# Split-buffer pairs and raw tiles of a weight stream: three and six, or four and four

## The chip, the cores and the metric

The kernel runs on one core of one Trainium2 chip. The metric is the device time of one execution in microseconds, the median of the runs shown.

## The reference

One layer of a hybrid trunk works on two request groups that share the weights: 128 context tokens and 256 latent tokens, 384 token columns of width 2048 in all, in float32. Cut to what matters:

```python
mod = silu(c) @ w_mod + b_mod                # one vector for each group, 6 x 2048 columns
h = rmsnorm(x, g) * (1 + sc_a) + sh_a        # modulated by parts of mod
parts = h @ w_in                             # 16,944 columns: three branches and their gates
merged = g0 * (y_m @ w_br_m) + g1 * (y_r @ w_br_r) + g2 * (y_s @ w_br_s)   # mLSTM, retention, SSD
x = x + g_a * (merged @ w_out)
h = rmsnorm(x, g) * (1 + sc_f) + sh_f
x = x + g_f * (square(relu(h @ w_ff1)) @ w_ff2)   # width 8192
y = rmsnorm(x, final_norm_g)
```

The three scans (y_m, y_r, y_s) also return their final states for the context group.

## The kernel before

Every large product streams its weights from HBM in raw tiles of 128 partitions x 1024 float32 values (512 KB). A weight is split in two halves that TensorE takes at its fast rate: whi is the rounded weight (`rnd`, line 88, ScalarE), wlo is what rounding left (`tt`, line 91, VectorE: raw minus whi). The activations are split in the same way, and each product is three matmuls (high by high, high by low, low by high; lines 201 to 203 and 209 to 211).

The work is a list of units (`unit_list`), filled by `strip` (line 114): a unit is one raw tile of weights, 4 row blocks by 256 columns (kind A, 24 matmuls of 384 columns) or 2 row blocks by 512 columns (kind B5, 18 matmuls of 512 columns). Four to eight units, two for the branch matrices, make a block that fills PSUM banks and is evacuated one unit later (`flush_evac`). Two further streams run in the background. `bg` holds generators for the scans, one step after each unit. And w_mod, whose parts for later stages aren't needed at the start, is mixed into the same list: `strip` adds `tune["rate"]` to a counter for each unit and, each time the counter passes 1, puts a modulation tile (kind M) behind the unit, 128 in all. Eight of them make a quarter of one part of mod (512 columns), after which the counter is set back by 3 in place of 1. The rate is 0.65 in the first stage of `run_units` (lines 915 to 939, 25 tiles), between 0.25 and 0.65 from there to the end of the retention stage (31 tiles), 0.65 in the branch stage (line 1446, 44 tiles), 0.5 in w_out (10 tiles) and 0.8 at the start of w_ff1 (18 tiles).

A modulation tile isn't split. `mod_tile` (line 328) queues `first`, which adds two rows' worth of products to macc on VectorE (line 333; four instructions where `mx` is 2), and `second`, which takes the other products through ScalarE (line 342) and POOL (line 343, an addition to macc). Only the last of these sets the raw tile free (`raw_done`). At a quarter's end `mod_end` (line 350) sums macc on TensorE, and `mod_begin` puts a memset of macc (POOL) and the loads of the next bias (SP, line 321) in front of what is queued. `pop_mods` takes a few of these steps after each unit; a None in the queue ends its turn.

`run_units` (line 213) sets the order by hand, since every engine runs its instructions in the order of the program. For unit i it emits the splits of the units up to i + SPB - 1 (line 217), then issues raw tiles, then the unit's matmuls, a background step, modulation steps and evacuations. `emit_raws` (line 135) lists raws on the SP queue up to `pos["used"] + RAWB`, where `pos["used"]` is the first raw, in list order, that isn't free yet. Where a split needs a raw that isn't listed, `emit_splits` takes modulation steps until it is:

```python
while ri not in raws:      # lines 148 to 150
    pop_mods(1)
    emit_raws()
```

RAWB is also the number of buffers of the raw tiles (line 82), SPB that of whi and of wlo (lines 153 and 154). A buffer given to a new tile makes the new tile's first writer wait, on the chip, for the last reader of the one that was released first. A raw tile, a whi and a wlo have 4 KB per partition each.

Before `run_units` a start stage (lines 399 to 597) makes the modulated input and the third branch gate from 32 raw tiles of w_in and 32 tiles of w_mod of 1 MB (`mraw`, four buffers of their own), in groups; `st_half(i, 1)` emits a split ahead (line 511), and `st_split(0)` and `st_split(1)` come before the loop (lines 555 and 558).

Of the kernel before, what the change touches and what calls it, by code (L numbers as in the profile page):

```python
# [46 lines left out]
def hybrid_step(ctx: ExitStack, tc: tile.TileContext, cpack, x_prompt, x_sample, c, state_mlstm_C,  # L47
# [3 lines left out]
                final_norm_g, y_prompt, y_sample, new_C, new_n, new_m, new_ret, new_ssd):  # L51
    nc = tc.nc
    act, dve, pool, pe, sp = nc.scalar, nc.vector, nc.gpsimd, nc.tensor, nc.sync
    RAWB, SPB = 6, 3

    class Pool:
        def __init__(self, name, side="left", space=None):
# [20 lines left out]
    def gbank(name="gb"):  # L78
        return psum([128, 512], name, bufs=4, tag="g")
# [7 lines left out]
    def rnd(out, in_, **kw):  # L87
        act.activation(out=out, in_=in_, func=AF.Copy, **kw)  # L88

    def tt(eng, out, a, b, op):  # L90
        eng.tensor_tensor(out=out, in0=a, in1=b, op=op)  # L91
# [7 lines left out]
    def mm(out, l, r, start=True, stop=True):  # L99
        pe.matmul(out, l, r, start=start, stop=stop)  # L100
# [323 lines left out]
    def st_pump():  # L424
        while todo and held[todo[0][0]] < (4 if todo[0][0] == "m" else RAWB):
            kind, key, src, nk = todo.popleft()
            held[kind] += 1
            t = start([128, 2048], "mraw", bufs=4) if kind == "m" else raw_tile()
            sp.dma_start(out=r3(t, nk), in_=src.rearrange("(k p) f -> p k f", p=128))
            (mraw if kind == "m" else wraw)[key] = r3(t, nk)  # L430
# [6 lines left out]
    def st_gemv(g, m):  # L437
        if g >= NG:
            return
        n = groups[g][1]  # L440
        if m == 1:
            mps[g] = bank("gemv")
        o = 0 if m else 128 * n
        for hf in range(n):
            t = mraw.pop((g, m, hf))
            nk = KT // n
            for kk in range(nk):
                k = nk * hf + kk
                q = k % 4
                mm(mps[g][32 * q:32 * q + 32, o:o + 128 * n], cs[:, k], t[:, kk], k < 4, k >= 12)  # L450
            held["m"] -= 1
        if m == 0:
            p = mps.pop(g)
            mps[g] = macc[:, g % 2, 0:256 * n]
            act.copy(out=mps[g], in_=p[:, 0:256 * n])
            if g + 1 < NG:
                st_scale(g + 1)
        st_pump()
# [14 lines left out]
    def st_build(g):  # L473
        if g >= NG:
            return
        k0, n = groups[g]
        for k in range(k0, k0 + n):
            p = bank()
            for c_ in range(3):
                tp(p[:, 128 * c_:128 * c_ + 128], xt[:, c_, 128 * k:128 * k + 128])  # L480
            t = start([128, T], "ht", bufs=2)
            for v, a, b in GRP:
                if k % 2 or n == 1:
                    act.activation(out=t[:, a:b], in_=p[:, a:b], func=AF.Identity, scale=scA[:, k, v:v + 1],
                                   bias=shA[:, k, v:v + 1])
                else:
                    dve.tensor_scalar(out=t[:, a:b], in0=p[:, a:b], scalar1=scA[:, k, v:v + 1],
                                      scalar2=shA[:, k, v:v + 1], op0=ALU.mult, op1=ALU.add)
            rnd(hhi[:, k], t)
            tt(dve, hlo[:, k], t, hhi[:, k].bitcast(F32), ALU.subtract)  # L490

    def st_split(i, eng=dve):
        if i >= len(units):
            return
        g, u = units[i]
        n = groups[g][1]
        w = 1024 // n
        s_ = wraw.pop((g, u))
        hi = strm([128, n, w], "whi", bufs=SPB, dt=F32R)
        lo = strm([128, n, w], "wlo", bufs=SPB, dt=F32R)  # L500
        rnd(hi, s_)
        tt(eng, lo, s_, hi.bitcast(F32), ALU.subtract)
        wsp[i] = (hi, lo)
        held["w"] -= 1
        st_pump()

    def st_half(i, half):
        g, u = units[i]
        k0, n = groups[g]
        if half:  # L510
            st_split(i + 2)
        wh, wl = wsp[i]
        nc_ = 8 // n
        for c_ in range(nc_ // 2 * half, nc_ // 2 * half + nc_ // 2):
            p = gbank()[:, 0:T]
            q = slice(128 * c_, 128 * c_ + 128)
            for kk in range(n):
                k = k0 + kk
                mm(p, wh[:, kk, q], hhi[:, k], kk == 0, False)
                mm(p, wh[:, kk, q], hlo[:, k], False, False)  # L520
                mm(p, wl[:, kk, q], hhi[:, k], False, kk == n - 1)
            a = acc[:, nc_ * u + c_]
            if g == 0:
                act.copy(out=a, in_=p)
            elif n == 1 and c_ % 2:
                t = start([128, T], "at", bufs=2)
                act.copy(out=t, in_=p)  # L527
                tt(pool, a, a, t, ALU.add)
            else:
                tt(dve, a, a, p, ALU.add)  # L530
                if g == NG - 1:
                    act.activation(out=a, in_=a, func=AF.Sigmoid)
# [23 lines left out]
    st_vec(0)  # L556
    st_build(0)
    st_split(1)
    def st_m1(g):
        st_gemv(g, 1)  # L560

    def st_m0(g):
        st_gemv(g, 0)

    nxt = {1: {0: (st_m1, st_m0), 1: (st_vec, st_build)}, 2: {1: (st_m1,), 3: (st_m0,), 4: (st_vec,), 5: (st_build,)}}
    i = 0
    for g, (k0, n) in enumerate(groups):
# [21 lines left out]
        for h_ in range(4 * n):  # L589
            if g == NG - 1 and h_ in (4, 6):  # L590
                g_prep(h_ // 2 - 2)
            st_half(i + h_ // 2, h_ % 2)
            if later_loads:
                later_loads.popleft()()
            for f in nxt[n].get(h_, ()):
                f(g + 1)
# [1140 lines left out]
```

## Time and profile before

| | us |
|---|---|
| median of 3 runs | 2814.65 |
| the runs | 2812.88 to 2815.4 |
| the profiled execution | 2816.29 |
| its span, from the first to the last instruction | 2814.5 |

The profile is of one execution. Times are us from the start of the span. Engines: PE is TensorE's matmul, PEld its weight load, DVE VectorE, ACT ScalarE, POOL GpSimd, SP the queue that issues the transfers (SPq its sequencer). A row names a line of the kernel, an operation, the tiles written and read, and in brackets or behind `<-` what ended the idle time before it. TensorE's mean granted clock is 0.993 of full speed.

### The profile page before, as it was taken

The page shows a single profiled execution, that of the slowest core. Times are in us where ns is not written, and L with a number is a line of the kernel's source. Part 1 is how long each engine was busy: PE and PEld are TensorE (multiplying, and loading weights), DVE is VectorE, ACT ScalarE, POOL GpSimd, SP SyncE. Part 2 cuts the span into 40 slices and gives each one's busy share as a digit, 9 for nine tenths or more (in the row PEclk, how much of TensorE's full clock was granted, in tenths as well). Part 3 has the DMA queues.
Part 4 walks back from the last instruction along what each step waited for, and adds up shares of the span by engine and source line. Part 5 has one row for each costly group of instructions (what it writes and reads, how often), then busy time and mean ns, then how long its engine had stood idle before and what let it go on. Part 6 is the DMA issues. An engine that isn't in the chain of part 4 may idle for free. (4 is left out here: it accounts for less than half of the span.)

```text
span 2814.5 us, 38093 instructions
## 1 busy us (share of the span) xinstructions
PE 2725.1 (97%) x15023; PEld 2501.5 (89%) x15023; DVE 1561.0 (55%) x1883; ACT 1155.5 (41%) x1708; POOL 754.8 (27%) x588
## 2 busy tenths in 40 slices
PE   6999999999999999999999998999999999999998
PEld 5899988899998988989999877988899899889987
DVE  3666566645765465567876756773343334334434
ACT  5333444546643343544444445452233233323333
POOL 3200233512251111235766442441100100010012
PEclk9999999999999999999999999999999999999999
DMA  9955555545755555466666653664443344344442
GB/s 316 293 194 173 149 170 158 168 141 154 213 151 158 154 179 166 142 191 205 195 201 188 226 161 115 187 203 140 129 127 128 128 128 127 128 128 127 127 144 103
DMA packets 377835, 465.54 MB, mean 165 GB/s; under 512 B 20980, under 2 KB 277128, under 8 KB 376504
## 3 DMA queue, kind: packets, MB, share of 16 engines
q1 hardware_dynamic: 377656, 463.10, 53.8%
q8 instruction: 118, 1.93, 0.3%
q14 instruction: 61, 0.50, 0.1%
HBM read 449.47 MB, written 13.57 MB: 165 GB/s over the span
## 5 line engine op out<-in xcount | busy, mean ns | idle before, releaser
L91 DVE TENSOR_TENSOR wlo<-raw,whi 128x1024 fp32r<-128x1024 f32 x599 | 819.5, 1373 | 955.3 <-ACT whi L88 946.1
L88 ACT ACTIVATE whi<-raw 128x1024 fp32r<-128x1024 f32 x600 | 632.5, 1058 | 1005.8 <-PE sb L100 465.6
L100 PE MATMUL gb<-hhi,whi 128*128 128x384 f32 x1600 | 552.1, 345 | 13.5 <-ACT at L527 5.3
L100 PE MATMUL gb<-hhi,wlo 128*128 128x384 f32 x1600 | 541.3, 338 | 11.8 <-DVE wlo L91 11.7
L100 PE MATMUL gb<-hlo,whi 128*128 128x384 f32 x1600 | 538.8, 337 | 0.0
L91 POOL TENSOR_TENSOR macc<-macc,raw 128x512 f32<-128x512 f32 x194 | 324.1, 1670 | 354.0 <-issue 247.1
L100 PE MATMUL gb<-h2l,whi 128*128 128x384 f32 x1024 | 344.5, 336 | 5.1 <-DVE h2l L1544 5.0
L100 PE MATMUL gb<-h2i,wlo 128*128 128x384 f32 x1024 | 344.1, 336 | 4.1 <-DVE wlo L91 4.1
L100 PE MATMUL gb<-h2i,whi 128*128 128x384 f32 x1024 | 344.1, 336 | 2.2 <-ACT h2i L1540 1.5
L333 DVE SCALAR_TENSOR_TENSOR macc<-raw,cs,macc 128x512 f32<-128x512 f32 x318 | 326.0, 1033 | 7.0 <-DMA macc<-in_b_mod_dram 1.1
L100 PEld LDWEIGHTS gb<-hhi,whi 128*128 128x128 f32 x1600 | 303.4, 190 | 29.3 <-issue 8.4
L100 PEld LDWEIGHTS gb<-hhi,wlo 128*128 128x128 f32 x1600 | 303.1, 189 | 17.7 <-DVE wlo L91 17.6
L100 PEld LDWEIGHTS gb<-hlo,whi 128*128 128x128 f32 x1600 | 303.1, 189 | 1.3 <-issue 0.5
L91 POOL TENSOR_TENSOR x<-x,t 128x512 f32<-128x512 f32 x45 | 71.7, 1623 | 801.7 <-DVE t L91 801.7
L100 PEld LDWEIGHTS gb<-h2l,whi 128*128 128x128 f32 x1024 | 193.2, 189 | 8.0 <-DVE h2l L1544 7.9
L100 PE MATMUL gb<-whi,ahi 128*128 128x512 f32 x512 | 199.3, 389 | 0.0
L100 PE MATMUL gb<-wlo,ahi 128*128 128x512 f32 x512 | 199.3, 389 | 0.0
L100 PE MATMUL gb<-whi,alo 128*128 128x512 f32 x512 | 199.2, 389 | 0.0
L100 PEld LDWEIGHTS gb<-h2i,wlo 128*128 128x128 f32 x1024 | 193.3, 189 | 5.7 <-DVE wlo L91 5.7
L100 PEld LDWEIGHTS gb<-h2i,whi 128*128 128x128 f32 x1024 | 193.3, 189 | 4.8 <-ACT h2i L1540 1.8
L342 ACT ACTIVATE raw<-raw,cs 128x512 f32<-128x512 f32 x194 | 133.8, 716 | 68.3 <-DVE macc L333 63.0
L100 PE MATMUL gb<-yhi,whi 128*128 128x384 f32 x384 | 129.1, 336 | 1.3 <-ACT yhi L88 1.3
(413 smaller groups left out, 3899.1 us busy)
## 6 DMA issues: line engine op xcount, KB each, us to landing
raw<-in_w_in_dram SPq DMA_DIRECT2D x264, 512.0 KB
raw<-in_w_ff_dram SPq DMA_DIRECT2D x256, 512.0 KB
raw<-in_w_mod_dram SPq DMA_DIRECT2D x128, 512.0 KB
mraw<-in_w_mod_dram SPq DMA_DIRECT2D x32, 1024.0 KB
raw<-in_w_out_dram SPq DMA_DIRECT2D x32, 512.0 KB
raw<-in_w_br_r_dram SPq DMA_DIRECT2D x16, 512.0 KB
raw<-in_w_br_m_dram SPq DMA_DIRECT2D x16, 512.0 KB
raw<-in_w_br_s_dram SPq DMA_DIRECT2D x16, 512.0 KB
```

What stands on the lines that cost most here:

```text
L88: act.activation(out=out, in_=in_, func=AF.Copy, **kw)
L91: eng.tensor_tensor(out=out, in0=a, in1=b, op=op)
L100: pe.matmul(out, l, r, start=start, stop=stop)
L333: dve.scalar_tensor_tensor(out=macc[:, v], in0=t[:, kk], scalar=cs[:, 2 * r + kk, v:v + 1], in1=macc[:, v], op0=ALU.mult, op1=ALU.add)
L342: act.activation(out=t[:, kk], in_=t[:, kk], func=AF.Copy, scale=cs[:, 2 * r + kk, 1:2])
```

## The change

The weight stream gets four pairs of split buffers in place of three and four raw tiles in place of six: 2 x 4 + 4 tiles of 4 KB per partition as before 2 x 3 + 6. In the start stage the split made ahead is that of the unit i + 3 in place of i + 2, and one more split is made before the loop. `run_units` follows SPB by itself: it splits up to unit i + 3.

```diff
-    RAWB, SPB = 6, 3
+    RAWB, SPB = 4, 4
...
         if half:
-            st_split(i + 2)
+            st_split(i + 3)
         wh, wl = wsp[i]
...
     st_build(0)
     st_split(1)
+    st_split(2)
     def st_m1(g):
```

## Rows read from the trace of the kernel before

**Rows 1.** The page, part 1: busy us, share, instructions by engine.

```profile
PE 2725.1 (97%) x15023; PEld 2501.5 (89%) x15023; DVE 1561.0 (55%) x1883; ACT 1155.5 (41%) x1708; POOL 754.8 (27%) x588
```

**Rows 2.** TensorE's waits: releaser: us in total, times, longest.

```profile
PE gb L100 <- DVE wlo L91: 26.6, 30, 3.1
PE gb L100 <- ACT whi L88: 5.5, 5, 2.7
```

**Rows 3.** By stage: stretch, length, PE, PEld, DVE, ACT, POOL, PEclk, DMA share, GB/s.

```profile
284.00:455.00 171.00, 162.32 (x849) 147.38 (x848) 104.55 (x158) 77.84 (x125) 57.73 (x42) 0.99 0.56 163
455.00:566.00 111.00, 105.07 (x562) 98.14 (x561) 68.36 (x110) 55.28 (x92) 46.86 (x34) 0.97 0.54 156
1190.00:1572.00 382.00, 375.36 (x2206) 373.25 (x2206) 278.85 (x259) 178.48 (x250) 232.15 (x150) 1.00 0.63 194
1757.00:1892.00 135.00, 130.14 (x723) 124.22 (x722) 109.91 (x98) 70.02 (x99) 64.04 (x37) 1.00 0.65 194
```

**Rows 4.** SP's timeline, w_ff1 and w_ff2: start, length, engine, line, operation, tiles, count.

```profile
2049.58 12.90 SPq L139 DMA_DIRECT2D raw<-in_w_ff_dram  x4
...
2182.27 8.53 SPq L139 DMA_DIRECT2D raw<-in_w_ff_dram  x3
```

**Rows 5.** Waits of the SP queue: releaser: us in total, times, longest.

```profile
SPq L139 <- POOL macc L91: 300.8, 91, 8.9
```

**Rows 6.** Timeline: one modulation tile on three engines, the issue behind it.

```profile
1381.56 1.52 DVE L333 SCALAR_TENSOR_TENSOR macc<-raw,cs,macc 128x512 f32<-128x512 f32 x2
1382.33 1.51 ACT L342 ACTIVATE raw<-raw,cs 128x512 f32<-128x512 f32 x2 [2.44 <-DVE macc L333]
1383.19 3.76 POOL L91 TENSOR_TENSOR macc<-macc,raw 128x512 f32<-128x512 f32 x2 [1.97 <-issue]
1386.97 2.74 SPq L139 DMA_DIRECT2D raw<-in_w_in_dram  x2
```

**Rows 7.** Timeline: one modulation tile beside POOL work.

```profile
1392.57 3.49 DVE L333 SCALAR_TENSOR_TENSOR macc<-raw,cs,macc 128x512 f32<-128x512 f32 x2
1393.88 5.57 POOL L91 TENSOR_TENSOR macc<-macc,raw 128x512 f32<-128x512 f32 x3
```

**Rows 8.** Timeline: a raw tile's issue on SP, and the split waiting for it.

```profile
1395.54 0.37 SPq L139 DMA_DIRECT2D raw<-in_w_in_dram  x1
1399.54 1.06 ACT L88 ACTIVATE whi<-raw 128x1024 fp32r<-128x1024 f32 x1 [1.77 <-DMA raw<-in_w_in_dram]
```

**Rows 9.** Instructions on raw tiles: count: ns min/median/max, first, last start.

```profile
L88 ACT ACTIVATE whi<-raw x600: 1038/1061/1093, 22.1 to 2793.1; 128x1024 fp32r<-128x1024 f32 x150
L91 DVE TENSOR_TENSOR wlo<-raw,whi x599: 1206/1226/2334, 28.2 to 2794.2; 128x1024 fp32r<-128x1024 f32 x200
```

**Rows 10.** Branch stage: macc's, then whi's instructions, columns as in rows 3.

```profile
1190.00:1572.00 382.00, 11.05 (x96) 11.49 (x96) 102.96 (x88) 0.00 (x0) 153.24 (x90) 1.00 0.63 194
1190.00:1572.00 382.00, 346.90 (x1361) 245.73 (x1362) 134.10 (x85) 88.93 (x84) 0.00 (x0) 1.00 0.63 194
```

**Rows 11.** Timeline at a quarter's end, from one modulation tile to the next.

```profile
1408.90 1.53 DVE L333 SCALAR_TENSOR_TENSOR macc<-raw,cs,macc 128x512 f32<-128x512 f32 x2
1418.94 1.84 PE L100 MATMUL sb<-cp,macc 128*128 128x1 f32 x16
1425.58 0.95 POOL L326 MEMSET macc<- 128x1024 f32 x1
1426.56 0.55 SPq L321 DMA_DIRECT2D macc<-in_b_mod_dram  x2
1428.28 4.03 DVE L333 SCALAR_TENSOR_TENSOR macc<-raw,cs,macc 128x512 f32<-128x512 f32 x4 [1.05 <-DMA macc<-in_b_mod_dram]
```

**Rows 12.** TensorE's waits from 284 to 566 us.

```profile
PE gb L100 <- DVE wlo L91: 10.1, 10, 1.8
PE gb L100 <- ACT whi L88: 4.4, 3, 2.7
```

**Rows 13.** Busy time in the first 100 us, columns as in rows 3.

```profile
0.00:100.00 100.00, 73.36 (x674) 63.03 (x675) 41.99 (x69) 48.47 (x86) 44.37 (x43) 0.98 1.01 306
```

## The prediction

> **What bounds it now.** The first view is the page's busy shares: TensorE is busy for 2725.1 us, 97% of the span, so the other engines matter only where they make it wait [rows 1]. The second is TensorE's waits: 26.6 us in 30 waits end on the low half of a split weight (wlo, VectorE), 5.5 us in 5 on the high half (whi, ScalarE) [rows 2]. These 32.1 us are all that a deeper row of split buffers can give back. The third is busy time by stage [rows 3]. TensorE fills 375.36 of 382.00 us in the branch stage (1190 to 1572) and 130.14 of 135.00 us in the first columns of w_ff1, so both stages run at its pace; VectorE is busy for 278.85 and 109.91 us of them, and no engine but TensorE is full.
>
> That pace comes from the SP queue where no modulation tile is in the stream: a raw tile is issued each time a split frees one. Four issues of the w_ff1 part in 12.90 us are (12.90 - 0.37) / 3 = 4.18 us for a unit of kind A; three in 8.53 us of the w_ff2 part are 4.08 us for a unit of kind B5 [rows 4]. So three A units take TensorE 12.5 us.
>
> **What is moved.** No instruction is removed; st_split(2) comes earlier and every split one unit earlier. What changes is two windows. Splits are made for the units i to i+3 in place of i to i+2, and raws are listed up to pos["used"] + 4 in place of + 6. One raw of 512 KB stands for one unit, so the total in flight goes from 9 units to 8. That alone is harmless: without modulation tiles a raw is wanted four units (16.7 us) after the split that frees its buffer, and it needs 4.0 us to land (below). I cost the stretches without modulation tiles at nothing; the cover is those 16.7 us, and were it gone each unit could show up to 4.0 us.
>
> The modulation tile (M) is what counts. It holds a raw tile but uses no split buffer, and its raw is freed only when VectorE, ScalarE and POOL have taken it into macc. Walk emit_splits with 4 and 4: when the loop is at the unit behind an M, the split four places behind that M needs a raw that the list may not yet hold, since pos["used"] stands at the M. The loop in line 148 then pops first() and second() of this M on the spot. Following lines 114 to 158 over the 696 entries, this happens for all 128 M tiles (22 of them with 6 and 3). Each M is so placed on VectorE and ScalarE between the split three units ahead and the next one.
>
> The hardware then waits by release: a raw is issued when the fourth release before it, in program order, is done (before, the sixth). The SP queue waits so now: 300.8 us in 91 waits end on POOL's last addition of an M [rows 5]. Counting releases, an M at place m gates the raw at m+6, where it gated m+9 before. In the dense stages (0.65 M for each unit: a a M a M ...) the raw at m+6 is mostly a weight whose split stands, on VectorE, ahead of the next M but one. So a ring closes: M taken in, raw issued, landed, split, next M. Behind the split that waits for its raw, the evacuations of the PSUM blocks and the background pieces are queued on ScalarE and VectorE, and at a quarter's end the POOL memset and the bias transfer on SP; TensorE waits for these next.
>
> **The price of one turn.** One M from its first VectorE instruction to POOL's last: 1381.56 to 1383.19 + 3.76 = 1386.95, so 5.4 us, and SP issues the freed raw at 1386.97 [rows 6]. Beside POOL work the pair on VectorE takes 3.49 us in place of 1.52, and M lasts from 1392.57 to 1393.88 + 5.57 = 1399.45, 6.9 us [rows 7]. I take 6.0. Landing: issued at 1395.54, the waiting ScalarE starts at 1399.54, 4.0 us [rows 8]. Split: 1.06 us on ScalarE (median) [rows 9], and on VectorE 134.10 / 85 = 1.58 us in this stage [rows 10], between 1.23 and 2.33 [rows 9]. A VectorE pair of M: 2 x 102.96 / 88 = 2.34 us [rows 10].
>
> The Trainium skill (DMA: Bandwidth & Descriptors, section Anatomy of one DMA, on another issuing path) prices a transfer at about 2.0 us plus bytes over 436 GB/s, which would be 3.2 us for 512 KB; the row's 4.0 us decides, and by the page each wide step below would be 0.8 us shorter and the branch stage some 18 us cheaper.
>
> Two A units and an M (a wide step): 6.0 + 4.0 + 1.06 + 1.58 = 12.6 us. One A unit and an M (a narrow step): the next M follows one split later, 2.34 + 1.58 = 3.9 us. Together 16.5 us for three A units that take TensorE 12.5.
>
> A quarter is eight M (spacings wide, narrow, wide, narrow, wide, narrow, wide) and a gap, 15.4 A units in all: 15.4 x 4.18 = 64.4 us of TensorE. The ring: 4 x 12.6 + 3 x 3.9 = 62.1 us. Other work in the same queues: VectorE's 278.85 - 134.10 - 102.96 = 41.8 us over 84 units is 0.5 us each; ScalarE's 178.48 - 88.93 - 44 x 1.51 = 23.1 us is 0.3 us [rows 3, 6, 10]. Half of it should fall in waits: 0.4 us x 12 = 4.7 us. The gap at the quarter's end: M's 6.0, TensorE's sum 1.84, memset 0.95, the bias transfer (issue to VectorE's start) 1428.28 - 1426.56 = 1.7 us, 10.5 us; before it lasts 1428.28 - 1408.90 = 19.4 us at TensorE's pace, which has room [rows 11]. Sum 62.1 + 4.7 + 10.5 = 77 us, so 12.6 us over TensorE's 64.4.
>
> Ends: all at the short rows, 4 x (5.4 + 4.0 + 1.06 + 1.23) + 3 x (1.52 + 1.23) + 9.9 = 65 us, no loss; all at the long ones with the other work in full and the old gap, 4 x (6.9 + 4.0 + 1.06 + 2.33) + 3 x (3.49 + 2.33) + 9.4 + 19.4 = 103 us, a loss of 39. I stay with 12.6, nearest to the stage's means.
>
> **The sum by stage.**
> - Branch stage, 44 M, 5.5 quarters: 5.5 x 12.6 = +69 us (0 to +215).
> - w_ff1, 18 M at 0.8 for a unit: here a raw waits for a split two A units back, 4.0 + 1.06 + 1.58 = 6.6 us for each single A against 4.18. A quarter of 12.5 units (52.3 us) becomes about 3.9 + 5 x 6.6 + 12.6 + 10.5 = 60 us: 2.25 x 8 = +18 us (0 to +45).
> - First stage of run_units (284 to 566), 25 M among 46 units: TensorE has 282 / 46 = 6.1 us of work and waits for each [rows 3], above the ring's 77 / 15.4 = 5.0, so the mean doesn't bind. But its waits on splits are 10.1 + 4.4 us already [rows 12], and the forced M comes earlier in full queues. +10 us (-14, if all these waits go, to +40).
> - Retention: the three gate strips between (12 units) have M at 0.65, each of four VectorE instructions, 4 x 1.17 = 4.7 us in place of 6.0: 11.3 + 6.3 = 17.6 us a turn against 12.5. Two turns, of which the splits already made hide half: +5 us (0 to +12).
> - Elsewhere splits made earlier give back a part of the 32.1 - 14.5 us: -5 us (0 to -12).
> - Start: all 16 DMA engines are busy for the first 100 us (share 1.01) [rows 13], so a shallower row of raws costs no transfer time, and the w_mod tiles keep their four buffers. 0 (-4 to +5).
>
> Sum +97 us on the profiled execution's 2816.29 us (span 2814.5), 1.6 us above the runs' median: 2912, so about 2910 us.
>
> **Rivals.** Faster (1 in 10): the ring turns in under TensorE's time. The point is 12.5 us for a wide and a narrow step; at the short rows it is 11.7 + 2.8 = 14.5 for three units, and only the gap (9.9 in place of 19.4) brings the quarter to 65. Then the third unit of lookahead removes up to 32.1 us [rows 2]: 2783 to 2809 us. For it: the waits are there. Against it: 0.8 of a wide step is landing and macc work that no split buffer shortens. The Trainium skill (Perfetto Trace Analysis, section Optimization Strategy) says that a gap repeating on the busy engine can mean too few buffers for the next tile, which by itself speaks for the fourth pair; the trace agrees that the gaps are there (26.6 us on wlo), but the raws are buffers too.
>
> No difference (0.06): the fourth pair stays empty in the dense stages, since of four units one or two are M, and the ring is as fast as TensorE: 2809 to 2820 us.
>
> Much slower (1 in 10): VectorE beside POOL all the time, the long rows: 215 + 45 + 40 + 12 gives about 3125 us, from 3010 on.
>
> **How the numbers follow.** Forecast 0.74 at 2910 us. The range leaves out the faster case and the much slower one, 2 in 10: 2815 to 3010 us. A measurement of this kernel tells about 0.2% (5.6 us) from no change. Faster 0.10, same 0.06, slower 0.84.
>
> **What would show it.** Right: TensorE's waits on wlo and whi rise to over 60 us, nearly all in the branch stage and at the start of w_ff1; the branch stage lasts some 450 us; ScalarE's whi waits on the landing of raws, which wait on POOL's macc; the w_ff part without M keeps its 4.08 to 4.18 us a unit. Wrong: the branch stage keeps its 382 us with the SP queue issuing raws before an M ends, or the loss lies in the first 220 us.

## The result, and the profile after

| | before | after |
|---|---|---|
| median of 4 runs, us | 2814.56 | 2895.49 |
| the runs, us | 2812.88 to 2815.4 | 2891.35 to 2898.21 |
| the profiled execution, us | 2816.29 | 2897.05 |
| its span, us | 2814.5 | 2895.1 |
| TensorE's mean granted clock | 0.993 | 0.980 |

The ratio is 1.0283, with a 95% interval of 1.0271 to 1.0295: the change costs 81 us. The forecast was 2910 us with a range of 2815 to 3010.

The page of the kernel after, part 1, answers to [rows 1]: busy us, share, instructions by engine.

```profile
PE 2759.3 (95%) x15023; PEld 2527.2 (87%) x15023; DVE 1486.1 (51%) x1883; ACT 1163.0 (40%) x1708; POOL 670.2 (23%) x588
```

The same instructions run on every engine. TensorE's share falls from 97% to 95%, yet its busy time grows by 34.2 us; VectorE and POOL are busy for less. No other engine comes near a full span, so the loss should lie in waits (and in slower work on TensorE). The waits come next.

TensorE's waits in the kernel after, against [rows 2]: releaser: us in total, times, longest.

```profile
PE gb L100 <- DVE wlo L91: 27.3, 34, 1.6
PE gb L100 <- ACT whi L88: 25.8, 12, 6.0
PE sb L100 <- DVE Cb L91: 9.7, 4, 4.1
...
PE sb L100 <- POOL macc L91: 7.1, 8, 2.3
PE sb L100 <- POOL xd L91: 5.6, 2, 3.8
```

The fourth pair of split buffers didn't shorten the waits on splits: wlo keeps its 27 us and whi goes from 5.5 to 25.8. Waits on Cb and xd, tiles of the SSD scan in the background, grow from 2.8 us before to 15.3.

The waits of the SP queue after, against [rows 5], in the same columns.

```profile
SPq L139 <- POOL macc L91: 414.4, 95, 12.3
```

Raw tiles wait 114 us longer than before on POOL's last addition of a modulation tile (M), in about as many waits.

Where the time went is best read by stage. This table is worked out from the traces: each stage runs from TensorE's first weight matmul in it to that of the next one. Before in us, then the difference of each kernel to it. The lower lines belong to the experiments. Each line is of one profiled execution.

```
                 start  mLSTM    sx   SSD   ret. branch w_out w_ff1a  rest  span
before           224.8  344.9 107.6 171.2  351.0  374.5 154.5  152.9 933.0 2814.5
after             -1.4   +6.9  -0.8 +13.6   +0.7  +37.8  +6.4  +16.0  +1.3  +80.6
e1_raw4_pair3     +4.4  +20.1  +1.9  -1.7   +0.6  +57.4 +14.9  +14.5  +4.9 +117.0
e3_raw5_pair3     -0.4   +4.2   0.0  -0.5   -0.1   +6.7  +1.6   +4.8  -0.6  +15.7
e4_no_mod_raw     +8.9   -4.0  -0.8  +2.2   -2.2   +9.4  -0.6   -1.2  +4.8  +16.6
e5_short_mod_44   +0.8   -8.4  -0.8 +12.9   -1.2   +4.4  +1.0   +8.9  +0.4  +18.1
e6_short_mod_63   -1.3  -10.4   0.0  -0.7   -0.1   -1.1  -5.4   -5.7  -0.6  -25.2
e8_long_mod_44    +0.7  +54.5  -0.8 +13.4   -1.3 +143.4 +40.0  +47.1 +10.9 +308.0
e7_rate_44        +1.8   +6.5  +8.6 +19.0   -1.2   -2.9  +0.6  +12.6  +7.1  +52.2
e2_order          -0.8   +7.9   0.0  +6.4   -1.2   +5.7  -3.4   +3.4  -0.6  +17.4
e9_late_44        -1.0  +21.9  +0.9  -1.8   -0.3  +35.2 +13.0  +13.5  +3.1  +84.5
e10_late_short_44 +0.4   -3.5  +1.0  -1.8   -0.2   +6.9  +1.7   +8.6  +0.5  +13.4
```

mLSTM is the first stage of `run_units` (rate 0.65), sx the columns without M behind it, SSD the strip beside the SSD scan, ret. the gate strips and the retention stage, w_ff1a the columns of w_ff1 that carry M. The loss lies where M is dense (mLSTM, branch, w_out, w_ff1a: 67.1 us) and in the SSD strip (13.6 us). Where no M is in the stream (sx, most of the rest) nothing changed, and in the retention stage, with 24 M at a lower rate for the most part, hardly anything (+0.7).

Busy time in the branch stage (same work) of the kernel before, then of the kernel after: stretch, length, PE, PEld, DVE, ACT, POOL, PEclk, DMA share, GB/s.

```profile
1199.00:1574.00 375.00, 368.36 (x2156) 366.25 (x2157) 273.99 (x255) 173.41 (x235) 225.07 (x142) 1.00 0.62 192
```

```profile
1219.00:1631.00 412.00, 385.87 (x2150) 377.27 (x2149) 243.22 (x256) 173.44 (x233) 181.57 (x142) 0.96 0.56 174
```

TensorE's idle time in the stage goes from 375.00 - 368.36 = 6.6 to 26.1 us, 19.5 more, and its busy time for the same matmuls grows by 17.5 us, at a granted clock of 0.96 in place of 1.00. Together they are the 37 us.

What ScalarE's instruction for whi, the first of a split, waited for in this stage shows where its pace comes from (releaser: us in total, times, longest). Before:

```profile
ACT whi L88 <- PE gb L100: 112.0, 41, 4.8
ACT whi L88 <- DMA raw<-in_w_br_m_dram: 8.9, 5, 3.6
```

After:

```profile
ACT whi L88 <- DMA raw<-in_w_in_dram: 39.1, 18, 5.1
ACT whi L88 <- DMA raw<-in_w_br_s_dram: 20.8, 9, 4.7
ACT whi L88 <- DMA raw<-in_w_br_m_dram: 19.0, 9, 4.8
ACT whi L88 <- DMA raw<-in_w_br_r_dram: 15.2, 7, 4.7
ACT whi L88 <- PE gb L100: 8.1, 2, 4.3
```

Before, a split waited for TensorE to set a pair free, for 112.0 us, and for landings of raws for some 15 us; after, it waits 94.1 us for landings and 8.1 us for TensorE. The stage now runs at the pace of the raws. What that costs depends on their pace: with the short M below, splits wait 198 us for landings here, and the stage loses 4.4 us.

One turn of the ring, in rows picked from the timelines of four engines of the kernel after: start, length, engine, line, operation, count, and in brackets the idle time before and what ended it.

```profile
1474.99 1.53 DVE L333 SCALAR_TENSOR_TENSOR macc<-raw,cs,macc 128x512 f32<-128x512 f32 x2
1475.77 1.51 ACT L342 ACTIVATE raw<-raw,cs 128x512 f32<-128x512 f32 x2 [1.95 <-DVE macc L333]
1477.18 1.04 ACT L88 ACTIVATE whi<-raw 128x1024 fp32r<-128x1024 f32 x1
1478.26 2.11 DVE L91 TENSOR_TENSOR wlo<-raw,whi 128x1024 fp32r<-128x1024 f32 x1 [1.74 <-ACT whi L88]
1480.30 1.53 DVE L333 SCALAR_TENSOR_TENSOR macc<-raw,cs,macc 128x512 f32<-128x512 f32 x2
...
1482.06 2.65 POOL L91 TENSOR_TENSOR macc<-macc,raw 128x512 f32<-128x512 f32 x2 [2.77 <-issue]
1484.75 1.45 SPq L139 DMA_DIRECT2D raw<-in_w_in_dram  x2
1488.57 1.06 ACT L88 ACTIVATE whi<-raw 128x1024 fp32r<-128x1024 f32 x1 [3.45 <-DMA raw<-in_w_in_dram]
1489.66 1.23 DVE L91 TENSOR_TENSOR wlo<-raw,whi 128x1024 fp32r<-128x1024 f32 x1 [3.86 <-ACT whi L88]
1490.80 1.53 DVE L333 SCALAR_TENSOR_TENSOR macc<-raw,cs,macc 128x512 f32<-128x512 f32 x2
```

This is the chain that the prediction drew. The M of 1480.30 is taken in until 1482.06 + 2.65 = 1484.71; SP issues a raw at 1484.75; it lands and the waiting ScalarE starts at 1488.57, 3.8 us later; its split follows, and the next M starts on VectorE at 1490.80, a wide step of 10.5 us. The narrow step is the upper half: from 1474.99 to 1480.30, 5.3 us.

The start of the next quarter, in rows picked from four engines.

```profile
1463.69 2.63 DVE L333 SCALAR_TENSOR_TENSOR macc<-raw,cs,macc 128x512 f32<-128x512 f32 x2
...
1523.94 1.53 DVE L333 SCALAR_TENSOR_TENSOR macc<-raw,cs,macc 128x512 f32<-128x512 f32 x2
...
1528.33 1.97 PE L100 MATMUL sb<-cp,macc 128*128 128x1 f32 x14 [0.93 <-POOL macc L91]
1529.90 2.94 POOL L91 TENSOR_TENSOR mg<-mg,sg 128x384 f32<-128x384 f32 x2 [1.63 <-DVE sg L91]
1532.79 0.95 POOL L326 MEMSET macc<- 128x1024 f32 x1
1533.77 0.54 SPq L321 DMA_DIRECT2D macc<-in_b_mod_dram  x2
1535.19 1.54 DVE L333 SCALAR_TENSOR_TENSOR macc<-raw,cs,macc 128x512 f32<-128x512 f32 x2 [0.92 <-DMA macc<-in_b_mod_dram]
```

From the first M of one quarter to the first of the next it takes 1535.19 - 1463.69 = 71.5 us: 60.25 us for the eight M and 11.25 us for the gap. It is one of five whole quarters of the stage. Their starts, read in the same way from each trace, are 70.1 to 76.1 us apart after, 72.83 in the mean, and 64.2 to 67.2 us before, 66.05 in the mean. So a quarter loses 6.8 us, and the stage 5.5 x 6.8 = 37 us; the table shows 37.8.

### The profile page after: what moved, and what is told of

Its sections match the earlier page's. It is cut to its first block, busy times and chain, and to the rows that moved or that the text cites. A ratio compares the mean times of both kernels' runs of the same rounds, so it can differ in the third digit from the quotient of the medians.

```text
span 2895.1 us, 38180 instructions
## 1 busy us (share of the span) xinstructions
PE 2759.3 (95%) x15023; PEld 2527.2 (87%) x15023; DVE 1486.1 (51%) x1883; ACT 1163.0 (40%) x1708; POOL 670.2 (23%) x588
## 5 line engine op out<-in xcount | busy, mean ns | idle before, releaser
L91 POOL TENSOR_TENSOR macc<-macc,raw 128x512 f32<-128x512 f32 x194 | 254.4, 1311 | 566.8 <-issue 396.7
L333 DVE SCALAR_TENSOR_TENSOR macc<-raw,cs,macc 128x512 f32<-128x512 f32 x318 | 255.4, 811 | 9.9 <-DMA macc<-in_b_mod_dram 4.3
```

Of the source, the lines that this page charges most:

```text
L333: dve.scalar_tensor_tensor(out=macc[:, v], in0=t[:, kk], scalar=cs[:, 2 * r + kk, v:v + 1], in1=macc[:, v], op0=ALU.mult, op1=ALU.add)
```

## The experiments

The theory: an M holds its raw tile until POOL is done with it, and with four raws, a raw a few places further on can't be issued before; the ring of M, issue, landing and split is longer than TensorE's work. The rivals: the lost raws as such (too few transfers under way, M or no M), and the order of the instructions (a split one unit further ahead, and the M that it forces, stand in front of other work).

### Fewer raw tiles alone

```diff
-    RAWB, SPB = 6, 3
+    RAWB, SPB = 4, 3      # e1_raw4_pair3
+    RAWB, SPB = 5, 3      # e3_raw5_pair3
```

> Four raw tiles and three pairs of split buffers: the raw half of the change alone. Ring theory (an M tile frees the raw six places on, whatever the number of pairs): the branch stage loses about 40 us and the start of w_ff1 about 18 as with the whole change, while the SSD stage (ga/sz, 676 to 840 us of before), where the whole change lost 17 us, loses under 6, since with three pairs the first half of M is again placed behind the background step; total about 2814 + 65 = 2880 us. Rival (the pairs do it: splits waiting for buffers ahead of other work): no loss, about 2815 us.

> Five raw tiles and three pairs, one size between. Ring theory: an M then frees the raw seven or eight places on, so the branch stage loses between 0 and 20 us; total 2815 to 2845 us. Rival (the pairs do it): 2815 us within 6.

Four raws and three pairs took 2939.51 us, a ratio of 1.0439 (1.0424 to 1.0455), well over what was expected and slower than the change itself. Five raws and three pairs took 2832.22 us, 1.0062 (1.0047 to 1.0077). So the raws are the loss: beside three pairs the sixth is worth 18 us, the fifth another 107 us. The fourth pair is a gain of 44 us beside four raws (2939.51 to 2895.49), though the change as a whole loses. With three pairs the branch stage looks like this, in the columns as above.

```profile
1225.00:1657.00 432.00, 392.56 (x2151) 380.52 (x2150) 244.92 (x258) 174.76 (x233) 187.29 (x142) 0.95 0.53 166
```

It is 20 us longer than with four pairs and four raws. By the program's order, a split that needs a free pair waits for TensorE, and the M queued behind that split on VectorE waits too, so TensorE's own progress enters the ring. The trace bears this out: whi waits for TensorE here for 47.1 us, where it was 8.1 in the kernel after.

```profile
ACT whi L88 <- PE gb L100: 47.1, 12, 11.4
```

The trace shows a second thing as well: 8 of the 44 M last 7.5 to 8.5 us, where none lasts over 5.4 in the kernel after; in each of the eight, POOL's additions stand behind pieces of an evacuation (mg or sg). No run tells the shares of the two. In the SSD strip the kernel loses nothing (-1.7), so that the 13.6 us there come from the fourth pair and the order that it brings, not from the raws.

### M without a raw tile

```diff
-    RAWB, SPB = 4, 4
+    RAWB, SPB = 3, 4
...
-                raw_list.append((mod_src(*m[:3]), 2))
-                unit_list.append((Block("M", m, None, KT), len(raw_list) - 1, 0, 1))
+                unit_list.append((Block("M", m, None, KT), None, 0, 1))
...
-                dve.scalar_tensor_tensor(out=macc[:, v], in0=t[:, kk], ...
+                dve.scalar_tensor_tensor(out=macc[:, v], in0=still_in, ...
-                act.activation(out=t[:, kk], in_=t[:, kk], ...
+                act.activation(out=t[:, kk], in_=still_in, ...
```

> Three raw tiles and four pairs; an M tile has no raw and no load: its instructions on VectorE, ScalarE and POOL are the same in number, operation and size but read a constant column, so mod gets wrong values (this part of the computation is left out). Ring theory: with M out of the ring the branch stage is back at TensorE's pace (380 us or less in place of 422) and w_ff1's start at 125 in place of 141, though there are fewer raw tiles than ever; total 2780 to 2815 us. Rival (fewer weights in flight is what costs): slower than the changed kernel, above 2895 us.

It took 2832.22 us, 1.0056 (1.0040 to 1.0073), 17 us above the interval that was expected and far from the rival's time. With only three raws the branch stage loses 9.4 us in place of 37.8, w_ff1a nothing (-1.2) and the SSD strip 2.2 in place of 13.6 (no split forces an M here): most of the loss needs M to have a raw in the list. M's transfers are gone too (DMA share 0.41 in the branch stage, for 0.56 in the change), which this run doesn't tell from the hold; the short M below keeps them. Three raws aren't harmless as such: the start loses 8.9 us and the rest 4.8, in stretches that the change itself leaves alone. What is left in the branch stage (9.4) wasn't taken apart.

### A shorter, a longer and a rarer M

In the short M all four products run on VectorE, nothing on ScalarE and POOL (`mx` 2 everywhere); it is put into the change and into the kernel before. In the long M, POOL does each addition to macc twice. In the third kernel M comes every second unit in the branch stage, and ten fewer there.

```diff
-    tune = {"bg": 1, "rate": 0.0, "due": 0.0, "pops": 3, "mx": 0}
+    tune = {"bg": 1, "rate": 0.0, "due": 0.0, "pops": 3, "mx": 2}
...
-    tune.update(rate=0.65, pops=2, mx=0)
+    tune.update(rate=0.65, pops=2, mx=2)    # both: e5_short_mod_44, e6_short_mod_63
...
-                tt(pool, macc[:, 1], macc[:, 1], t[:, kk], ALU.add)
+                for _ in range(2):              # e8_long_mod_44
+                    tt(pool, macc[:, 1], macc[:, 1], t[:, kk], ALU.add)
...
-    tune["rate"] = 0.0
+    tune["rate"] = 0.45                     # e7_rate_44, columns of sx
...
-    tune.update(rate=0.65, pops=2, mx=0)
+    tune.update(rate=0.5, pops=2, mx=0)     # e7_rate_44, branch stage
```

> Four raws and four pairs, but every M tile is taken in by four VectorE instructions alone (mx = 2 in every stage): its raw is free after about 3.0 us in place of 4.4 to 5.2. Ring theory: a wide step falls from some 10.8 to 9.4 us and a quarter of the branch stage from 71.5 us to TensorE's 64, so that stage loses 0 to 10 us against before in place of 38; the start of w_ff1, where a raw waits for a split two units back, keeps half of its 16; the SSD stage, where nothing changes, keeps its 14; total 2840 to 2865 us. Rival (fewer weights in flight, whatever M takes): 2885 us or more; VectorE has 66 us more work in the branch stage, which would make it worse.

> The same shortening of M with six raws and three pairs, as the control. Ring theory: with six raws the ring has room, so the time stays within 10 us of 2814; the difference of this run and the one with four raws is 25 to 50 us in place of 81. Rival (M's length is a cost of its own): a gain of the size of the run with four raws, 30 us or more, here as well.

> Four raws and four pairs; POOL makes each of M's additions twice (mod gets wrong values), so that the 97 tiles that POOL takes part in hold their raw about 2.7 us longer. POOL is busy for 23% of the span and never ends TensorE's work by itself. Ring theory: four wide steps and the gap of each quarter grow by 2.7 us or more: the branch stage loses another 60 to 80 us, the start of w_ff1 another 15 to 30, the first stage 10 to 40; total 2985 to 3040 us. Rival (POOL's part of M is off the path): 2895 to 2910 us.

> Four raws and four pairs; the branch stage has one M tile for each two units (a a M throughout, 34 tiles in place of 44) and nine tiles go into the convolution columns that had none. Ring theory: with a a M throughout an M gates the next M but one and no weight, so the branch stage loses 0 to 8 us against before in place of 38; the convolution columns pay 0 to 8 us for theirs; total 2850 to 2870 us. Rival (each M in the stream has its price wherever it stands, as all 128 are still taken in at once): 2885 to 2900 us, with the branch stage at 30 or more.

Short M with four raws and four pairs: 2835.94 us, 1.0073 (1.0058 to 1.0088), 4 us below what was expected. That is 60 us less than the change, but the short M is a gain with six raws and three pairs too (2790.89 us, below). Against that kernel, with the same M, the change of buffers costs 45 us in place of 81, so 36 us of the loss hang on M's length. In the branch stage it costs 4.4 + 1.1 = 5.5 us in place of 37.8, in mLSTM 2.0 in place of 6.9. The other losses don't shrink so: 13.6 us in the SSD strip as before, 6.4 in w_out as before, and 8.9 + 5.7 = 14.6 for 16.0 in w_ff1a. Long M: 3121.63 us, 1.1085 (1.1068 to 1.1101), more than expected. Branch stage with the short M, then with the long one, in the same columns:

```profile
1203.00:1582.00 379.00, 369.94 (x2152) 365.77 (x2151) 270.40 (x341) 117.83 (x150) 65.92 (x58) 1.00 0.60 189
```

```profile
1266.00:1784.00 518.00, 422.72 (x2153) 407.62 (x2152) 280.36 (x257) 173.90 (x233) 326.55 (x226) 0.88 0.43 138
```

Two more additions on POOL, whose mean in this kernel is in the following group of its page (count, busy, mean ns, idle before), lengthen each of 44 M.

```profile
L91 POOL TENSOR_TENSOR macc<-macc,raw 128x512 f32<-128x512 f32 x388 | 587.9, 1515 | 492.9 <-issue 304.5
```

That is 2 x 1.515 = 3.0 us more work for an M. From VectorE's first instruction to POOL's last an M of this stage lasts 8.8 us, 4.6 in the kernel after (means of 44): 4.2 us more, where 2.7 were expected. The stage grew by (143.4 - 37.8) / 44 = 2.4 us for each. POOL is busy for 326.55 of 518 us, so it isn't full; its time counts because M stands in the ring. Nor is it so that POOL never ends TensorE's waits: on macc they are 7.1 us in the kernel after. An engine with a low share of busy time helps to set the pace of the stage.

Rarer M: 2867.72 us, 1.0183 (1.0167 to 1.0198), within the interval expected. With a regular a a M the branch stage has no loss (-2.9), although each M still holds a raw until POOL is done. Ten M fewer alone don't explain that: at 37.8 / 44 = 0.86 us each they are 9 us of the 40.7. The M that were moved cost elsewhere: 8.6 us in sx, 7.1 in the rest, where two M now fall in w_ff2; the SSD strip loses 19.0. The timelines of this kernel, for one M and what its release issues, show what became of the ring:

```profile
1455.49 2.28 DVE L333 SCALAR_TENSOR_TENSOR macc<-raw,cs,macc 128x512 f32<-128x512 f32 x2
1457.93 2.67 POOL L91 TENSOR_TENSOR macc<-macc,raw 128x512 f32<-128x512 f32 x2 [1.49 <-issue]
1460.63 0.37 SPq L139 DMA_DIRECT2D raw<-in_w_mod_dram  x1
1463.21 1.53 DVE L333 SCALAR_TENSOR_TENSOR macc<-raw,cs,macc 128x512 f32<-128x512 f32 x2
```

POOL is done with M at 1460.60 and SP issues at once, as in the change, but the raw that it issues at 1460.63 is of w_mod: in the list a a M a a M a a M the sixth raw behind an M is the second M behind it. The next M starts at 1463.21, before that raw can have landed, so it doesn't depend on it; the ring closes over two periods (four units, 16.7 us) and fits. In the change the raw behind an M was mostly a weight (w_in at 1484.75), whose split stands ahead of the next M or the next but one. Followed through the program's order, 40 of the 44 M of the branch stage gate a weight in the change, and 4 of the 34 here. So the loss hangs on which raw lies six places behind an M, as the prediction's counting of releases has it, and not on M's load on the engines alone.

The short M with six raws and three pairs took 2790.89 us, 0.9911 (0.9894 to 0.9927): 24 us faster than the kernel before, where within 10 us was expected, and faster than all others here. Its waits of TensorE, as in [rows 2]:

```profile
PE gb L100 <- DVE wlo L91: 14.7, 19, 1.8
PE gb L100 <- ACT whi L88: 2.9, 3, 1.8
```

Of the 32.1 us that the fourth pair was to shorten [rows 2], 14.5 are gone without it. The gain lies in stages with M (mLSTM -10.4, w_out -5.4, w_ff1a -5.7). The expectation's two theories are both right in part: the cost of the change of buffers fell to 45 us, within the 25 to 50 of the ring theory, but M's length is also a cost of its own. That the kernel before has the ring in these stages too, at the edge, would fit; no run tells it from the work that ScalarE and POOL are relieved of.

### The order of the instructions

`e2_order` is the kernel before (six raws, three pairs) with each M taken in directly behind the next splits, ahead of the background step, as the change forces it. `e9_late_44` is the change with the fourth unit's split behind the background step instead of ahead of the unit's matmuls, so that the forced M comes behind it too. `e10_late_short_44` is that with the short M.

```diff
             emit_splits(i + SPB)
+            if i and unit_list[i - 1][0].kind == "M":      # e2_order
+                while pos["used"] <= unit_list[i - 1][1]:
+                    pop_mods(1)
...
-            emit_splits(i + SPB)
+            emit_splits(i + SPB - 1)                       # e9_late_44, e10_late_short_44
...
             bg_steps(tune["bg"])
+            emit_splits(i + SPB)
+            emit_raws()
```

> Six raw tiles and three pairs as before, but each M tile is taken in as soon as the loop is at the unit behind it, right behind the splits and ahead of the background step, as the whole change forces it. Ring theory with an effect of order: the branch stage and w_ff1 keep their time within 5 us each (six raws leave room), the SSD stage loses about 15 us because VectorE gets M ahead of the scan's pieces; total 2815 to 2835 us. Rival (order is the whole loss): the branch stage loses about 40 us, total about 2890 us. Rival (order costs nothing): 2815 us within 6.

> Four raws and four pairs, with the split of unit i+3, and with it the M tile that it forces, emitted behind unit i's matmuls and background step in place of ahead of them. Theory of order for the SSD stage (VectorE and ScalarE get M and the split before the scan's pieces, and TensorE's next scan matmul waits): that stage loses 0 to 4 us against before in place of 14. Ring theory: the branch stage, which has hardly any background pieces, keeps its loss of 35 to 45 us, the start of w_ff1 its 14 to 18; total 2875 to 2890 us. Rival for the SSD stage (four raws are too few there too): it keeps 10 us or more, total 2895 us.

> Both at once: four raws and four pairs, the split of unit i+3 and its M behind the background step, and M on VectorE alone (mx = 2 throughout). If ring and order are the two causes and add up: the SSD stage within 4 us of before, the branch stage within 6, the start of w_ff1 6 to 10 us slower (its raws wait for splits, not for M), the first stage 5 to 10 faster; total 2810 to 2828 us against 2791 with six raws and three pairs. Rival (something else in the change costs): 2832 us or more, as without the later place.

`e2_order` took 2833.0 us, 1.0064 (1.0049 to 1.0079): M's place by itself costs 18 us, 6.4 of it in the SSD strip, where about 15 was expected, and 5.7 in the branch stage, just over the 5 expected. So M's place alone, with three pairs, is less than half of the strip's 13.6 us. `e9_late_44` took 2901.8 us, 1.0307 (1.0290 to 1.0324). Its SSD strip has no loss (-1.8 for +13.6), as expected, with the fourth split and its M both behind the background step, and the branch stage keeps its own (35.2). The sum missed the expectation of 2875 to 2890: mLSTM (+21.9) and w_out (+13.0) lost more than in the change. M now stands behind the background pieces, which may make the ring there longer; no run isolates it. `e10_late_short_44` took 2828.38 us, 1.0049 (1.0034 to 1.0064), at the upper end of what was expected. With M short and the order mended, four and four is still 37 us slower than six and three with the same short M: 8.0 us of it are in the branch stage, 6.9 in mLSTM, 7.1 in w_out and 14.3 in w_ff1a.

How the order acts in the SSD strip is plain on VectorE. First the kernel after, with TensorE's matmuls that wait at the end; then the kernel before at the same place of the scan.

```profile
714.83 2.98 DVE L333 SCALAR_TENSOR_TENSOR macc<-raw,cs,macc 128x512 f32<-128x512 f32 x4
717.73 1.22 DVE L91 TENSOR_TENSOR wlo<-raw,whi 128x1024 fp32r<-128x1024 f32 x1
718.86 1.22 DVE L91 TENSOR_TENSOR Cb<-Cb,cbm 128x1024 f32<-128x1024 f32 x1
...
720.23 2.85 PE L100 MATMUL sb<-Cb,xd 128*64 128x128 f32 x28 [4.10 <-DVE Cb L91]
```

```profile
707.76 1.22 DVE L91 TENSOR_TENSOR Cb<-Cb,cbm 128x1024 f32<-128x1024 f32 x1
708.90 0.68 DVE L91 TENSOR_TENSOR ti<-sb,EB 128x512 f32<-128x512 f32 x1
709.50 3.88 DVE L333 SCALAR_TENSOR_TENSOR macc<-raw,cs,macc 128x512 f32<-128x512 f32 x3
```

After, the forced M (2.98 us) and a split (1.22 us) run ahead of the scan's Cb, and TensorE waits 4.10 us for it; before, Cb runs first and M behind it. In `e9_late_44` Cb is again ahead of M:

```profile
727.11 1.22 DVE L91 TENSOR_TENSOR Cb<-Cb,cbm 128x1024 f32<-128x1024 f32 x1
728.85 4.68 DVE L335 SCALAR_TENSOR_TENSOR macc<-raw,cs,macc 128x512 f32<-128x512 f32 x4
```

## Why the prediction was right in sum, and where its steps failed

The direction held, and so did the mechanism in the branch stage, which is the largest term. The time lies 15 us below the forecast, nearer than the terms deserve, and that is luck: 31 us too many in the branch stage are for the most part cancelled by 25 us too few in the SSD strip, in w_out and in what was to be given back elsewhere.

**Branch stage, +69 forecast, +37.8 measured.** The mechanism was right, the loss of a quarter too high: 6.8 us for 12.6. The eight M take 59.3 us in the mean for 62.1 + 4.7 = 66.8, the gap 13.5 for 10.5, and TensorE's pace, taken as 64.4 us from 15.4 units, was 66.05 before, since TensorE has more to do there than the units (2156 matmuls in the stage, of which 84 units are 2016).

M was taken at 6.0 us from one free and one disturbed M of the kernel before [rows 6, 7]; in the ring it took 4.4 us (1480.30 to 1484.71; 4.3 to 5.4 over the stage), for the most part less than both, since VectorE has little to do while POOL adds. The split of the wide step was taken at 1.06 + 1.58 us; here VectorE is alone and it took 1490.80 - 1488.57 = 2.2 us. The landing was right: 3.8 us for 4.0 [rows 8]. So a wide step in the quarter shown is 10.4 to 11.3 us, not 12.6. The narrow step failed the other way: 5.3 us for 3.9, because whi stands behind M's products on ScalarE (1475.77, 1477.18), which the step left out. The gap shown, 11.25 for 10.5, is near by luck: M is 1.7 us shorter there, but the memset on POOL stands some 2.5 us behind an evacuation (mg at 1529.90), which the sum had not; the five gaps of the stage last 11.3 to 16.5 us. Mean durations of a stage were used for a chain that, once it is the bound, runs on engines that idle: that is the general mistake.

**The SSD strip, in "elsewhere" at -5, measured +13.6.** The prediction saw that every M would be forced between two splits, and that in the first stage this puts M earlier in full queues, but for the SSD strip it priced only raws and waits on splits. The experiments on the order put this on the fourth unit's split, with the M that it forces, ahead of the background step: behind it the loss is gone (`e9_late_44`, -1.8), and without a forced M most of it (`e4_no_mod_raw`, +2.2).

**w_ff1, +18 forecast, +16.0 measured; first stage, +10 and +6.9; start, 0 and -1.4.** The numbers are right within 3.1 us each. For w_ff1 the sum isn't borne out, though: with M at 3.0 us in place of 6.0 in its wide step and its gap it would give (8 - 6) x 2.25 = 4.5 us, an estimate, and the short M leaves 14.6. **Retention, +5 and +0.7:** it was to be half hidden by the splits already made; what hides the rest was not tested. **w_out, +6.4:** ten M that had no term.

**What would show it.** TensorE's waits on wlo and whi were to exceed 60 us, nearly all in the branch stage and w_ff1: they are 53.1 us, 10.8 of them in the branch stage and 11.3 in w_ff1. The branch stage was to last some 450 us and lasted 412.3. Part of the loss is not in waits at all: TensorE was busy 17.5 us longer there for the same matmuls, at a granted clock of 0.96; the prediction, with the clock at 1.00 in [rows 3], had not allowed for it. SP's waits on POOL's macc rose, whi waits on the landing of raws, and the stretch without M kept its time (+1.3), as said.

**The rivals.** Faster needed three A units and their M in 12.5 us; a wide and a narrow step take 10.5 + 5.3 = 15.8 in the turn shown. The fourth pair does give something back, 44 us beside four raws, but not the waits of the kernel before. The Trainium skill (Perfetto Trace Analysis, section Optimization Strategy) reads a repeated gap on the busy engine as possibly too few buffers; the runs agree with that, if one asks which buffers: raws count (beside three pairs the fifth is worth 107 us), and so does how long one is held (the short M, -24 us with no buffer more).

**What stays open.** Whether the lower clock added time in the branch stage or only filled waiting time of the ring: splits waited for TensorE for only 8.1 us there and for raws for 94.1, which speaks for the second, but no run sets the clock. What is left in the branch stage (4.4 to 9.4 us) with a short M or without its raw. And what costs 14 us in w_ff1a and 6 to 7 in w_out whatever M's length.

## What to carry to other kernels

When buffers move from one stage of a pipeline to another, find the consumer that holds a buffer longest and walk the ring that it closes (hold, issue, landing, next consumer) in time of undisturbed instructions; busy shares don't show it, since POOL was busy for 23% here, and of each microsecond by which its additions lengthened M over half was paid in the branch stage (2.4 of 4.2 us). Shortening that hold can be worth more than any split of the buffers: here it gave 24 us with six and three, and no split of the buffers that was tried gave any. And a lookahead that is made ahead of other work in an in-order queue moves all that it forces ahead of that work, so look at what it overtakes. To put it behind all background work was no gain in sum here (2901.8 us for 2895.49): the SSD strip lost its cost, mLSTM and w_out got one.

## What was not expected of the hardware

VectorE and POOL slow each other, and the ring takes part of that away, which the prediction didn't assume. The same additions to macc on POOL, and the products of M on VectorE, in the groups of the page of the kernel before, then after (count, busy, mean ns, idle before):

```profile
L91 POOL TENSOR_TENSOR macc<-macc,raw 128x512 f32<-128x512 f32 x194 | 324.1, 1670 | 354.0 <-issue 247.1
L333 DVE SCALAR_TENSOR_TENSOR macc<-raw,cs,macc 128x512 f32<-128x512 f32 x318 | 326.0, 1033 | 7.0 <-DMA macc<-in_b_mod_dram 1.1
```

```profile
L91 POOL TENSOR_TENSOR macc<-macc,raw 128x512 f32<-128x512 f32 x194 | 254.4, 1311 | 566.8 <-issue 396.7
L333 DVE SCALAR_TENSOR_TENSOR macc<-raw,cs,macc 128x512 f32<-128x512 f32 x318 | 255.4, 811 | 9.9 <-DMA macc<-in_b_mod_dram 4.3
```

Means fall by a fifth on both, with the same instructions on the same data, and they overlap less: of the 318 products on VectorE 177 run beside no POOL instruction before and 271 after, at a mean of 0.75 us in both kernels, where the others take 1.39 and 1.17 us. The Trainium skill (SBUF — State Buffer, section Who interferes with whom) has these two engines share one pair of ports under an exclusive lock; the rows agree in direction.

TensorE's granted clock was lower where TensorE waited more: its mean was 0.993 before, 0.980 in the change and 0.950 with the long M, where the branch stage had 0.88 and TensorE was busy for 422.72 us with matmuls that take 368.36 us before.
